# A diffusion layer on one core: the last bank in two halves, its second half squared on VectorE, epsilon as a column of the sums, and the mean's factor moved into the final norm's weights

## The chip, the core and the metric

The kernel runs on one core of one Trainium2 chip. The metric is the time of one execution in device microseconds, from the launch on the device to its end; lower is better. The profile's span runs from the first to the last instruction of the program and is a little shorter than that time.

## The reference, cut to what matters

One layer of a hybrid diffusion backbone on 256 latent tokens and 256 context tokens of width 2048 in float32: a SwiGLU feed-forward half step, a mixer (attention and mLSTM heads), a second feed-forward half step for the latent tokens, and a final RMS norm. The change touches the end of the second half step and the final norm alone:

```
D_MODEL = 2048; SEQ = 256; D_FF = 5632; RMS_EPS = 1e-6

def rms_norm(x, g):
    xf = x.astype(jnp.float32)
    y = xf * lax.rsqrt(jnp.mean(xf * xf, axis=-1, keepdims=True) + RMS_EPS)
    return (y * g.astype(jnp.float32)).astype(x.dtype)

def half_step_ffn(x, mod, i, g, w_up, w_down):
    h = adaln(x, g, mod, i)
    a, b = jnp.split(h @ w_up, 2, axis=-1)
    return x + 0.5 * mod[:, i + 2, None, :] * ((jax.nn.silu(a) * b) @ w_down)

    ...
    xl = half_step_ffn(xl, mod_l, 6, g_norm[l, 2], w_ffn2_up[l], w_ffn2_down[l])
    return rms_norm(xl, g_final)
```

## The kernel before

Every float32 matrix product is made of three products of rounded parts (`mm3`, L148 to L152). Each operand is split into a part `hi`, rounded by a ScalarE copy, and a rest `lo`, which VectorE gets by subtracting. TensorE then adds hi times hi, lo times hi and hi times lo in one PSUM bank. Weights arrive in tiles of 128 partitions by 2048 columns (1 MB, 8 KB per partition) and are split in two halves of 1024 columns (`split`, L120): L128 is the ScalarE copy, L129 the VectorE subtraction. There are three buffers for raw weights and four for each of hi and lo, so a split runs up to four halves ahead of TensorE. A buffer that TensorE has not yet read holds the split up, and a raw buffer that VectorE has not yet read holds up the next load on the DMA queue of SP.

The second feed-forward step works on 11 blocks of 512 hidden columns. The up projection of eight of them is done in the fast form `quad` (L2076 to L2175, banks X and Y) with chains of accumulating DMAs, issued by GpSimd, into the tiles `chain2` and `ra`. The down projection `down` adds pairs of blocks to `acc2`, a tile of 128 partitions, two token tiles and 2048 columns. Up and down are interleaved by hand (`sequence`, L2241). The order within an engine is otherwise made by a scheduler, which may move an instruction ahead of others unless it is pinned (`pin`, L337). An engine works through its instructions strictly in the order that is built.

When the last quad has used its chains, `before_final` (L2251) reuses their two buffers: `g8`, the gate row, and `gf`, the final norm's weights, each broadcast from one row to all 128 partitions by a DMA on SP (L2254, L2255). `gf` waits until the last split of the chain that lay in its buffer is done.

The end is `last2` (L2277). It loads the last block's down weights, four tiles of 2048 columns, and splits them (L2284 to L2290). Then for each of two token tiles `t` and each of four column blocks `cb` of 512:

- TensorE fills one bank with 12 products (`block`, L2200: four groups of 128 hidden columns, three products each), 512 columns wide.
- VectorE multiplies the bank by the gate (`half_gated`, L1030) and adds it to `acc2` (L2325).
- ScalarE squares the sum with an accumulator (`sumsq`, L163), which gives one column of the tile's four sums.
- VectorE multiplies the column block before it by `gf` (`gain`, L2293).

`ended` (L2295) closes a token tile: VectorE adds the four sums (L2298), multiplies by 1/2048 and adds epsilon (L2300), GpSimd raises to the power -1/2 (L2301), and ScalarE and VectorE scale the four column blocks (L2310, L2308; the very last one on VectorE with its gain, L2306). SP writes each block out (L2311). The first token tile's ending is laid between the banks of the second.

Of the kernel before, what the change touches and what calls it, by code (L numbers as in the profile page):

```python
# [9 lines left out]
F32 = mybir.dt.float32  # L10
# [3 lines left out]
AF = mybir.ActivationFunctionType  # L14
ALU = mybir.AluOpType
# [4 lines left out]
P = 128  # L20
D = 2048
# [25 lines left out]
CB = 512  # L47
NCB = D // CB
EPS = 1e-6
# [9 lines left out]
def tile_layer(ctx: ExitStack, tc: tile.TileContext, I: dict, out: bass.AP):  # L59
    nc = tc.nc  # L60
# [4 lines left out]
    sm = ctx.enter_context(pool(name="sm", bufs=2))  # L65
# [7 lines left out]
    def bank():  # L73
        return ps["mm"].tile([P, 512], F32, tag="mm", name="mm")

    def tbank():
        return ps["tr"].tile([P, 512], F32, tag="tr", name="tr")
# [20 lines left out]
    mhalf = cst.tile([P, 16], F32, name="mhalf")  # L98
# [17 lines left out]
    def raw_tile(n=2048):  # L116
        t = wp.tile([P, 2048], F32, tag="raw", name="raw", bufs=3)
        return t if n == 2048 else t[:, :n]
# [22 lines left out]
    def load_split(src, n=2048):  # L141
        raw = raw_tile(n)
        nc.sync.dma_start(raw, src)
        wt = split(raw, n)
        next(beside["load"], None)
        return wt
# [14 lines left out]
    def sumsq(dst, x, n=512):  # L161
        junk = sm.tile([P, 512], BF16, tag="junk", name="junk", bufs=1)
        scalar[0].activation(junk[:, :n], x, AF.Square, accum_out=dst)  # L163
# [173 lines left out]
    def pin(ins):  # L337
        tc.keep_in_program_order(ins)
# [58 lines left out]
    def drain(it):  # L397
        for _ in it:
            pass
# [62 lines left out]
    with pool(name="st", bufs=1) as st:  # L462
# [42 lines left out]
        def squares(s, t):  # L505

            ss4 = sm.tile([P, 4], F32, tag="ss4", name="ss4", bufs=4)
            for cb in range(NCB):
                xc = xs0[s, t][:, cb * CB : (cb + 1) * CB]
                if cb >= 2:  # L510
                    vector[0].scalar_tensor_tensor(junk[:, :CB], xc, 1.0, xc, op0=ALU.mult, op1=ALU.mult, accum_out=ss4[:, cb : cb + 1])
                else:
                    sumsq(ss4[:, cb : cb + 1], xc)
            return ss4

        def factor(ss4):
            s1 = sm.tile([P, 1], F32, tag="s1", name="s1")
            vector[0].tensor_reduce(s1, ss4, axis=AX.X, op=ALU.add)
            r = sm.tile([P, 16], F32, tag="rstd", name="rstd", bufs=4)[:, :1]
            vector[0].tensor_scalar(r, s1, 1.0 / D, EPS, op0=ALU.mult, op1=ALU.add)  # L520
            nc.gpsimd.tensor_tensor(r, r, mhalf[:, :1], op=ALU.pow)
            return r
# [91 lines left out]
        ss = squares(CTX, 0)  # L614
# [11 lines left out]
        r = factor(ss)  # L626
        for n, (s, t) in enumerate(((CTX, 1), (LAT, 0), (LAT, 1))):
            ss = squares(s, t)
# [4 lines left out]
            last, r = r, factor(ss)  # L633
# [98 lines left out]
    with pool(name="f1u", bufs=1) as f1u:  # L732
# [26 lines left out]
        for f in range(NPRE, FB):  # L759
            pab = []  # L760
            for ab in range(2):
                wt = load_split(I["w_up1"][f - NPRE, ab])
                b = bank()
# [168 lines left out]
        halves = [cBh[:, q, :] for q in range(2)]  # L932
# [95 lines left out]
    def half_gated(a, y, g, sign=1.0):  # L1028

        nc.vector.scalar_tensor_tensor(a, y, 0.5 * sign, g, op0=ALU.mult, op1=ALU.mult)  # L1030
# [8 lines left out]
    LAST = [(CTX, cb) for cb in (1, 3, 0, 2)] + [(LAT, cb) for cb in (2, 0, 3, 1)]  # L1039
# [207 lines left out]
    parts = [load_split(I["w_c"][g]) for g in range(2)]  # L1247
# [7 lines left out]
    with ExitStack() as mx:  # L1255
# [146 lines left out]
        def conv(b, ch, ns):  # L1402

            y = m1.tile([P, 512], F32, tag="cy", name="cy", bufs=3)[:, : ns * T]
            nc.scalar.activation(y, b, AF.Identity, scale=cwT[:, ch, 2:3], bias=cbT[:, ch : ch + 1])
            b3 = b.rearrange("p (s t) -> p s t", s=ns)
            y3 = y.rearrange("p (s t) -> p s t", s=ns)
            for j in (0, 1, 3, 4):
                o = j - 2
                src = slice(max(o, 0), T + min(o, 0))  # L1410
                dst = slice(max(-o, 0), T + min(-o, 0))
                nc.vector.scalar_tensor_tensor(y3[:, :, dst], b3[:, :, src], cwT[:, ch, j : j + 1], y3[:, :, dst], op0=ALU.mult, op1=ALU.add)  # L1412
            return y
# [39 lines left out]
        for h in range(NH):  # L1453
            b = bank()
# [4 lines left out]
            y = conv(b, 8 + h, 2)  # L1459
# [77 lines left out]
        for h in range(NH):  # L1537
            b = bank()[:, :T]
# [6 lines left out]
            y = conv(b, h, 1)  # L1545
# [11 lines left out]
        for w in range(2):  # L1557
            gs = gains[:, w, :].rearrange("p (a b d) -> p a b d", a=2, b=2)
            for t in range(2):
                nc.vector.tensor_tensor(rt[:, w, t, 0, :], rope[:, t, 0, :], gains[:, w, :], op=ALU.mult)  # L1560
                for b in range(2):
# [4 lines left out]
                        op=ALU.mult,  # L1566
# [315 lines left out]
        for cb in range(NCB):  # L1882
# [8 lines left out]
            c = slice(cb * CB, (cb + 1) * CB)  # L1891
# [36 lines left out]
    with f2x:  # L1928
# [4 lines left out]
        def sab_tile():  # L1933
            return f2.tile([P, CB], F32, tag="sab", name="sab")
# [22 lines left out]
        for f in range(NPRE, FB):  # L1957
            pab = []
            for ab in range(2):
                wt = load_split(I["w_up2"][f - NPRE, ab])  # L1960
                b = (tbank() if f == FB - 1 else bank())[:, :T]
# [17 lines left out]
        acc2 = f2b.tile([P, 2, D], F32, name="acc2", bufs=1)  # L1979
# [4 lines left out]
        LAST = NF // FB - 1  # L1984
# [212 lines left out]
                                nc.scalar.activation(sab[t], bs[t], AF.Silu)  # L2197
                    yield

        def block(b, n, wt, t, first=True, last=True):  # L2200

            tt = slice(t * P, (t + 1) * P)
            for j in range(FB):
                w = slice(j * CB, (j + 1) * CB)
                mm3(b, hids[n][0][:, j, tt], hids[n][1][:, j, tt], *wt(w), first and j == 0, last and j == FB - 1)
            return b

        late = {}
# [42 lines left out]
        def before_final():  # L2251
            late["g8"] = f3.tile([P, D], F32, tag="c0", name="g8")
            late["gf"] = f3.tile([P, D], F32, tag="c1", name="gf")
            nc.sync.dma_start(late["g8"], mod_rows[8][LAT, :].partition_broadcast(P))  # L2254
            nc.sync.dma_start(late["gf"], I["g_final"].partition_broadcast(P))  # L2255

        def quads():
            for n in QUADS:
                yield from quad(n)
# [17 lines left out]
        def last2():  # L2277

            parts = []
            for cb in range(NCB):  # L2280
                if cb >= 2:
                    parts.append(load_split(I["w_dn2"][LAST, cb]))
                    continue
                raw = raw_tile()  # L2284
                nc.sync.dma_start(raw, I["w_dn2"][LAST, cb])
                hi = f3.tile([P, 2048], F32R, tag=f"f{2 * cb}", name=f"hi{cb}")
                lo = f3.tile([P, 2048], F32R, tag=f"f{2 * cb + 1}", name=f"lo{cb}")
                nc.scalar.activation(hi, raw, AF.Copy)
                nc.vector.tensor_tensor(lo, raw, hi.bitcast(F32), op=ALU.subtract)
                parts.append(lambda w, hi=hi, lo=lo: (hi[:, w], lo[:, w]))  # L2290
            def gain(t, cb):
                a = acc2[:, t, cb * CB : (cb + 1) * CB]
                pin(nc.vector.tensor_tensor(a, a, late["gf"][:, cb * CB : (cb + 1) * CB], op=ALU.mult))  # L2293

            def ended(t, ss):  # L2295

                s1 = sm.tile([P, 1], F32, tag="s1", name="s1")
                pin(nc.vector.tensor_reduce(s1, ss, axis=AX.X, op=ALU.add))  # L2298
                r = sm.tile([P, 16], F32, tag="rstd", name="rstd", bufs=4)[:, :1]
                pin(nc.vector.tensor_scalar(r, s1, 1.0 / D, EPS, op0=ALU.mult, op1=ALU.add))  # L2300
                nc.gpsimd.tensor_tensor(r, r, mhalf[:, :1], op=ALU.pow)  # L2301
                for cb in (0, 2, 1, 3):
                    c = slice(cb * CB, (cb + 1) * CB)
                    a = acc2[:, t, c]
                    if t and cb == 3:
                        pin(nc.vector.scalar_tensor_tensor(a, a, r, late["gf"][:, c], op0=ALU.mult, op1=ALU.mult))  # L2306
                    elif cb >= 2:
                        pin(nc.vector.tensor_scalar(a, a, r, None, op0=ALU.mult))  # L2308
                    else:
                        nc.scalar.activation(a, a, AF.Copy, scale=r)  # L2310
                    nc.sync.dma_start(out[t * P : (t + 1) * P, c], a)  # L2311
                    if not t and not cb:
                        yield


            sss = [sm.tile([P, 4], F32, tag="ss4", name="ss4", bufs=4) for _ in range(2)]
            first = ended(0, sss[0])
            for t in range(2):
                for cb in range(NCB):
                    c = slice(cb * CB, (cb + 1) * CB)  # L2320
                    b = block(bank(), LAST, parts[cb], t)
                    a = acc2[:, t, c]
                    y = sab_tile()
                    half_gated(y, b, late["g8"][:, c])
                    nc.vector.tensor_tensor(a, a, y, op=ALU.add)  # L2325
                    sumsq(sss[t][:, cb : cb + 1], a)
                    if cb or t:
                        gain(*divmod(4 * t + cb - 1, 4))
                    if t:
                        steps(first)  # L2330
            drain(ended(1, sss[1]))

        last2()


# [93 lines left out]
```

## Time and profile before

| what | us |
| --- | --- |
| median of three runs | 2601.55 (2598.96 to 2601.9) |
| the profiled execution, its own time | 2600.28 |
| its span, first to last instruction | 2598.0 |
| mean granted TensorE clock | 0.996 |
| last product of TensorE starts | 2588.19 |
| scaling of the last token tile starts | 2591.89 |
| first and last write of the output issued | 2584.45 and 2593.80 |

Times in the views are microseconds from the start of the span. In a line of the timeline stand the start, the duration, the engine, the source line, the operation, the tiles (written from read), the shape and the count; in square brackets how long the engine was idle before and what ended that. A line of the grouped view ends with the total busy time, the mean nanoseconds of one, and the idle time before them. A line of the stage view gives the stretch, its length, then for TensorE, its weight loads (PEld), VectorE (DVE), ScalarE (ACT) and GpSimd (POOL) the busy time and count, then the granted clock, the share of the DMA engines and their GB/s.

### The profile page before, as it was taken

The numbers are of one execution on the slowest core, as the hardware profiler recorded it, in microseconds if no ns is written. First come the engines' busy times: TensorE is split into PE (matmuls) and PEld (weight loads), VectorE is DVE, ScalarE is ACT, GpSimd is POOL, SyncE is SP. The second block draws the span as 40 slices with busy tenths as digits, with TensorE's granted clock in tenths as the row PEclk, the third lists the DMA queues.
The fourth block names the chain that finished last, engine by engine and source line by source line (L and its number), as shares of the span: only waits on it lengthen the run. The fifth ranks groups of instructions, "written<-read, shape, count | busy, mean of one in ns | idle before, by whom it ended". The sixth has DMA issues, their size and how long they took to land. (4 is left out here: it accounts for less than half of the span.)

```text
span 2598.0 us, 34128 instructions
## 1 busy us (share of the span) xinstructions
PE 2574.4 (99%) x12670; PEld 2145.3 (83%) x12670; DVE 2172.5 (84%) x2864; ACT 1419.1 (55%) x1822; POOL 216.1 (8%) x265
## 2 busy tenths in 40 slices
PE   8999999999999999999999999999999999999998
PEld 5788888888888888888889989888898888888887
DVE  7788888878888788888887888798889888887887
ACT  4454444544445565444454448456486676666664
POOL 0000000100000100000110000120000000000001
PEclk8999999999999999999999999999999999999999
DMA  9889999999999989989987897676768988989976
GB/s 391 346 220 265 269 286 268 263 276 285 262 287 262 281 246 242 218 216 224 229 254 261 296 321 242 235 279 215 267 239 244 276 267 259 271 275 275 260 230 174
DMA packets 127078, 680.51 MB, mean 262 GB/s; under 512 B 14136, under 2 KB 16696, under 8 KB 64832
## 3 DMA queue, kind: packets, MB, share of 16 engines
q1 hardware_dynamic: 98400, 492.73, 50.8%
q0 software_dynamic: 28512, 185.61, 36.5%
q8 instruction: 99, 1.62, 0.2%
q14 instruction: 67, 0.55, 0.1%
HBM read 660.39 MB, written 17.89 MB: 261 GB/s over the span
## 5 line engine op out<-in xcount | busy, mean ns | idle before, releaser
L128 ACT ACTIVATE hi<-raw 128x1024 fp32r<-128x1024 f32 (+2 forms) x500 | 519.0, 1042 | 424.2 <-PE mm L152 308.3
L129 DVE TENSOR_TENSOR lo<-raw,hi 128x1024 fp32r<-128x1024 f32 (+2 forms) x488 | 584.9, 1206 | 144.4 <-ACT hi L128 119.3
L128 ACT ACTIVATE hi<-chain 128x1024 fp32r<-128x1024 f32 x336 | 355.6, 1060 | 303.5 <-PE mm L152 191.4
L129 DVE TENSOR_TENSOR lo<-chain,hi 128x1024 fp32r<-128x1024 f32 x336 | 407.8, 1222 | 115.1 <-ACT hi L128 108.8
L152 PE MATMUL mm<-hi,hhi 128*128 128x512 f32 (+3 forms) x1024 | 394.0, 385 | 0.0
L152 PE MATMUL mm<-lo,hhi 128*128 128x512 f32 (+3 forms) x1024 | 387.0, 378 | 0.2 <-DVE lo L129 0.2
L152 PE MATMUL mm<-hi,hlo 128*128 128x512 f32 (+3 forms) x1024 | 386.4, 377 | 0.0
L208 DVE SCALAR_TENSOR_TENSOR junk<-sraw,cBh 128x1024 fp8e5<-128x1024 f32 x192 | 234.4, 1221 | 16.5 <-DMA sraw<-in_w_mt 14.3
L152 PEld LDWEIGHTS mm<-lo,hhi 128*128 128x128 f32 x1024 | 192.5, 188 | 34.5 <-DVE lo L129 0.6
L152 PEld LDWEIGHTS mm<-hi,hhi 128*128 128x128 f32 x1024 | 192.6, 188 | 31.0
L152 PEld LDWEIGHTS mm<-hi,hlo 128*128 128x128 f32 x1024 | 192.8, 188 | 30.7
L129 DVE TENSOR_TENSOR lo<-ra,hi 128x1024 fp32r<-128x1024 f32 x96 | 117.1, 1223 | 36.8 <-ACT hi L128 32.2
L128 ACT ACTIVATE hi<-ra 128x1024 fp32r<-128x1024 f32 x96 | 101.9, 1062 | 65.5 <-PE mm L152 49.0
L152 PE MATMUL mm<-lo,hid2h 128*128 128x512 f32 x352 | 137.1, 389 | 0.0
L152 PE MATMUL mm<-hi,hid2h 128*128 128x512 f32 x352 | 137.0, 389 | 0.0
L152 PE MATMUL mm<-hi,hid2l 128*128 128x512 f32 x352 | 136.9, 389 | 0.0
L152 PE MATMUL mm<-hi,sumshl 128*128 128x512 f32 x400 | 123.2, 389 | 0.0
L208 DVE SCALAR_TENSOR_TENSOR sr<-sr,cBl 128x1024 f32<-128x1024 f32 x84 | 102.2, 1224 | 15.1 <-DMA sr<-in_w_mt 13.6
L731 POOL DMA_DIRECT2D chain<-in_w_up1b x60 | 53.0, 884 | 729.4 <-DVE lo L129 729.4
L152 PE MATMUL mm<-hi,sumshh 128*128 128x512 f32 x352 | 108.4, 389 | 0.0
L152 PE MATMUL mm<-hhi,hi 128*128 128x512 f32 (+1 forms) x288 | 101.4, 352 | 0.0
L152 PE MATMUL mm<-hhi,lo 128*128 128x512 f32 (+1 forms) x288 | 99.0, 344 | 0.0
(490 smaller groups left out, 5457.0 us busy)
## 6 DMA issues: line engine op xcount, KB each, us to landing
raw<-in_w_dn SPq DMA_DIRECT2D x70, 1024.0 KB, 7.1
chain<-in_w_up1b POOLq DMA_DIRECT2D x60, 1024.0 KB, 10.2
sraw<-in_w_mt SPq DMA_DIRECT2D x96, 512.0 KB, 8.1
sr<-in_w_mt SPq DMA_DIRECT2D x81, 512.0 KB, 5.5
raw<-in_w_up1b SPq DMA_DIRECT2D x40, 1024.0 KB, 8.1
mraw<-in_w_m SPq DMA_DIRECT2D x32, 1024.0 KB, 8.1
raw<-in_w_up2b SPq DMA_DIRECT2D x32, 1024.0 KB, 8.1
chain<-in_w_dn POOLq DMA_DIRECT2D x30, 1024.0 KB, 8.5
```

Source lines behind the costliest of these rows:

```text
L128: scalar[0].activation(hi, src, AF.Copy)
L129: vector[0].tensor_tensor(lo, src, hi.bitcast(F32), op=ALU.subtract)
L152: tensor[0].matmul(out_ap, s, m, start=first and not n, stop=last and n == 2, skip_group_check=skip)
L208: ins = nc.vector.scalar_tensor_tensor(junk() if junk else raw, raw, 1.0, cB[s], op0=ALU.mult, op1=ALU.mult, accum_out=mT[:, i, s, kt, h : ...
L731: accum = lambda dst, src: nc.gpsimd.dma_start(dst, src, accum_op=ALU.add)
```

## The change

Four edits, all at the end.

- The last bank (second token tile, last column block) is filled as two banks of 256 columns, first columns 0 to 255, then 256 to 511, each with its own 12 products, gate and addition. The first half is squared by ScalarE as before. The second half is squared by VectorE, in one operation with an accumulator.
- The sums of a token tile have six columns instead of four. The fifth is the second half's sum (zero for the first token tile), the sixth holds 2048 times epsilon. GpSimd fills both by memsets, which the built program places at the start of GpSimd's instructions, between the two selects that make the identity.
- The step that multiplied by 1/2048 and added epsilon (L2300 before) is gone: the six columns are added and go straight to the power -1/2.
- The missing factor, the square root of 2048, is multiplied into `gf` by a ScalarE copy right behind its load in the code.

The additions to `acc2` are now pinned; on VectorE their order is the old one. The line numbers behind the edits move: L2325 becomes L2328, L2293 becomes L2294, L2298 becomes L2299, L2288 becomes L2289; L2301 to L2311 stay. The new lines are L2256 (the factor), L2318 and L2319 (the memsets), L2341 (VectorE's square).

```diff
-        def block(b, n, wt, t, first=True, last=True):
+        def block(b, n, wt, t, first=True, last=True, c0=0):
 
             tt = slice(t * P, (t + 1) * P)
             for j in range(FB):
-                w = slice(j * CB, (j + 1) * CB)
+                w = slice(j * CB + c0, j * CB + c0 + b.shape[1])
...
             nc.sync.dma_start(late["gf"], I["g_final"].partition_broadcast(P))
+            nc.scalar.activation(late["gf"], late["gf"], AF.Copy, scale=D ** 0.5)
...
                 r = sm.tile([P, 16], F32, tag="rstd", name="rstd", bufs=4)[:, :1]
-                pin(nc.vector.tensor_scalar(r, s1, 1.0 / D, EPS, op0=ALU.mult, op1=ALU.add))
-                nc.gpsimd.tensor_tensor(r, r, mhalf[:, :1], op=ALU.pow)
+                nc.gpsimd.tensor_tensor(r, s1, mhalf[:, :1], op=ALU.pow)
...
-            sss = [sm.tile([P, 4], F32, tag="ss4", name="ss4", bufs=4) for _ in range(2)]
+            sss = [sm.tile([P, 6], F32, tag="ss6", name="ss6", bufs=2) for _ in range(2)]
+            for ss in sss:
+                nc.gpsimd.memset(ss[:, 4:5], 0.0)
+                nc.gpsimd.memset(ss[:, 5:6], D * EPS)
             first = ended(0, sss[0])
+
+            def finished(t, cb, c0, n):
+                c = slice(cb * CB + c0, cb * CB + c0 + n)
+                b = block(bank()[:, :n], LAST, parts[cb], t, c0=c0)
+                a = acc2[:, t, c]
+                y = sab_tile()[:, :n]
+                half_gated(y, b, late["g8"][:, c])
+                pin(nc.vector.tensor_tensor(a, a, y, op=ALU.add))
+                return a
+
             for t in range(2):
                 for cb in range(NCB):
-                    c = slice(cb * CB, (cb + 1) * CB)
-                    b = block(bank(), LAST, parts[cb], t)
-                    a = acc2[:, t, c]
-                    y = sab_tile()
-                    half_gated(y, b, late["g8"][:, c])
-                    nc.vector.tensor_tensor(a, a, y, op=ALU.add)
-                    sumsq(sss[t][:, cb : cb + 1], a)
+                    halves = t == 1 and cb == NCB - 1
+                    a = finished(t, cb, 0, CB // 2 if halves else CB)
+                    sumsq(sss[t][:, cb : cb + 1], a, a.shape[-1])
                     if cb or t:
                         gain(*divmod(4 * t + cb - 1, 4))
+                    if halves:
+                        a = finished(t, cb, CB // 2, CB // 2)
+                        y = sab_tile()[:, : CB // 2]
+                        pin(nc.vector.scalar_tensor_tensor(y, a, 1.0, a, op0=ALU.mult, op1=ALU.mult, accum_out=sss[t][:, 4:5]))
                     if t:
                         steps(first)
```

## The prediction

> **What bounds the kernel now.** First the page, then the stage view (busy time by stretch), then the timelines of the end.
>
> ```profile
> PE 2574.4 (99%) x12670; PEld 2145.3 (83%) x12670; DVE 2172.5 (84%) x2864; ACT 1419.1 (55%) x1822; POOL 216.1 (8%) x265
> ```
> ```profile
> 2515.70:2588.60 72.90, 72.87 (x329) 59.93 (x327) 56.96 (x70) 32.63 (x42) 7.52 (x9) 1.00 0.63 188
> ```
>
> TensorE is busy for 99% of the span, and in the last 73 us before its end it is busy for 72.87 of 72.90 us. That stretch has no hole that could swallow a delay: what makes TensorE late before 2515 makes the end late by as much. After TensorE there is only a chain of small steps. Here it is on VectorE, then on ScalarE and GpSimd:
>
> ```profile
> 2586.62 0.69 DVE L2325 TENSOR_TENSOR acc<-acc,sab 128x512 f32<-128x512 f32 x1
> 2587.23 0.69 DVE L2293 TENSOR_TENSOR acc<-acc,gf 128x512 f32<-128x512 f32 x1
> 2588.61 0.69 DVE L1030 SCALAR_TENSOR_TENSOR sab<-mm,g 128x512 f32<-128x512 f32 x1 [0.70 <-PE mm L152]
> 2589.34 0.69 DVE L2325 TENSOR_TENSOR acc<-acc,sab 128x512 f32<-128x512 f32 x1
> ...
> 2590.88 0.16 DVE L2298 TENSOR_REDUCE s<-ss 128x1 f32<-128x4 f32 x1 [0.25 <-ACT junk L163]
> 2591.07 0.15 DVE L2300 TENSOR_SCALAR rstd<-s 128x1 f32<-128x1 f32 x1
> 2591.89 0.49 DVE L2308 TENSOR_SCALAR acc<-acc,rstd 128x512 f32<-128x512 f32 x1 [0.67 <-POOL rstd L2301]
> ```
> ```profile
> 2590.12 0.63 ACT L163 ACTIVATE junk<-acc 128x512 bf16<-128x512 f32 x1 [1.99 <-DVE acc L2325]
> 2590.66 0.19 ACT L163 ACTIVATION_READ_ACCUMULATOR junk<-acc 128x1 f32 x1
> ```
> ```profile
> 2591.30 0.55 POOL L2301 TENSOR_TENSOR rstd<-rstd,mhalf 128x1 f32<-128x1 f32 x1 [7.63 <-DVE rstd L2300]
> ```
>
> Read: the last bank is gated at 2588.61, added at 2589.34, squared by ScalarE at 2590.12, summed at 2590.88, given its mean and epsilon at 2591.07, raised to -1/2 at 2591.30. Only at 2591.89 can the last row be scaled and written out. A dependent VectorE step of 512 columns follows after 0.73 us (2588.61 to 2589.34), an independent one after 0.61 (2586.62 to 2587.23).
>
> **The end, part by part.** Can TensorE do the last bank as two halves at no cost?
>
> ```profile
> 2585.69 0.39 PE L152 MATMUL mm<-hi,hid2h 128*128 128x512 f32 x1
> ...
> 2588.19 0.39 PE L152 MATMUL mm<-lo,hid2h 128*128 128x512 f32 x1
> ```
> ```profile
> 1392.72 0.28 PE L152 MATMUL mm<-hi,hlo 128*128 128x256 f32 x1
> ...
> 1394.28 0.28 PE L152 MATMUL mm<-lo,hhi 128*128 128x256 f32 x1
> ```
>
> The bank's 12 products of 512 columns start 0.227 us apart (2.50 over 11). Elsewhere 14 products of 256 columns with the same weight loads start 0.120 apart (1.56 over 13). So 24 of them end at 2585.69 + 23 x 0.120 + 0.28 = 2588.73, 0.15 later than now (2588.58), and the first half at 2587.29. VectorE then works, in the order of the built program, through gate A, add A, gain of column block 2 (512 wide), gate B, add B, square B, sum.
>
> ```profile
> L1510 DVE SCALAR_TENSOR_TENSOR E<-mm,E 128x256 f32<-128x256 f32 x16 | 6.6, 415 | 0.7 <-POOL E L1495 0.6
> ```
> ```profile
> L129 DVE TENSOR_TENSOR lo<-raw,hi 128x1024 fp32r<-128x1024 f32 x464 | 563.9, 1222 | 137.3 <-ACT hi L128 112.3 <-PE mm L1429 9.9 <-PE mm L1705 1.7
> ...
> L208 DVE SCALAR_TENSOR_TENSOR junk<-sraw,cBh 128x1024 fp8e5<-128x1024 f32 x192 | 234.4, 1221 | 16.5 <-DMA sraw<-in_w_mt 14.3
> ...
> L208 DVE DVE_READ_ACCUMULATOR junk<-sraw,cBh 128x1 f32 x192 | 15.9, 83 | 0.0
> ```
>
> 256 columns take 0.415 us where 512 take 0.69, so each step shrinks by 0.27: 0.46 dependent, 0.34 independent. Gate A starts when the gain at 2587.23 lets go, 2587.84; add A 2588.30; gain 2588.64; gate B 2589.25 (its bank ended at 2588.73); add B 2589.71; square 2590.17; its accumulator is read 0.34 later and takes 0.08, so the sum starts at 2590.62 and ends at 2590.78. ScalarE's square of half A begins near 2588.7 and is long done. The step at L2300 is gone: POOL follows the sum 0.08 us later (now 2591.22 to 2591.30), takes 0.55, and scaling starts at 2591.45 instead of 2591.89. The end gains **0.44 us**. No row shows a 256-wide square with accumulator. If the halves saved nothing, the sum would come 0.27 x 5 later and the end lose 0.9; if the accumulator read were free, it would gain 0.5. I stay at the L1510 row, with 0.2 to 0.55 as its range.
>
> The Trainium skill, page "Vector Engine (DVE) Microarchitecture Reference", section "Points that are easy to get wrong", says that such an operation with two non-bf16 SBUF sources runs at half rate, no port being left for the accumulator. By it the square would take an estimated 0.27 us more and the gain be 0.17. The trace disagrees: with accumulator 1.221 us, L129 without one 1.222.
>
> **Epsilon.** Four one-column memsets appear on POOL, between the two selects that make the identity.
>
> ```profile
> 0.94 0.11 POOL L100 MEMSET mhalf<- 128x16 f32 x1
> ...
> 1.91 0.29 POOL L104 TENSOR_SCALAR_AFFINE_SELECT ident<-ident 128x128 f32<-128x128 f32 x1
> ```
> ```profile
> 2.98 0.28 PE L467 MATMUL tr<-ident,cc 32*128 32x32 f32 x1 [2.98 <-ACT cc L191]
> ```
>
> At 0.11 each they delay the identity from 2.20 to 2.64 at most. Its first user starts at 2.98 and waits for ScalarE. Cost nothing; without that cover, 0.44.
>
> **The factor in gf.** This is the term that decides. The new ScalarE instruction at L2256 stands, in the built program, behind the last copy of L2105 and ahead of six splits of L128, two of ra and four of raw. It waits for gf's load, which before nobody needed until 2576.
>
> ```profile
> L2255 SPq DMA_DIRECT2D gf<-in_g_final x1: 327/327/327, 2502.1 to 2502.1; - x1
> ...
> DMA to landing us min/median/max: 10.6/10.6/10.6
> ```
> ```profile
> 2506.39 0.60 ACT L2105 ACTIVATE ca<-X 128x512 f32<-128x512 f32 x1 [0.54 <-DVE cy L2077]
> 2508.93 1.06 ACT L128 ACTIVATE hi<-ra 128x1024 fp32r<-128x1024 f32 x1 [1.93 <-PE mm L152]
> ...
> 2553.40 1.92 ACT L2288 ACTIVATE hi<-raw 128x2048 fp32r<-128x2048 f32 x1 [2.03 <-DMA raw<-in_w_dn]
> 2555.22 1.99 ACT L128 ACTIVATE hi<-raw 128x1024 fp32r<-128x1024 f32 x2
> ```
> ```profile
> 2510.02 2.60 DVE L129 TENSOR_TENSOR lo<-ra,hi 128x1024 fp32r<-128x1024 f32 x2 [2.53 <-ACT hi L128]
> ```
> ```profile
> 2512.76 0.39 PE L152 MATMUL Y<-lo,h2hi 128*128 128x512 f32 x1
> 2512.99 0.39 PE L152 MATMUL Y<-hi,h2hi 128*128 128x512 f32 x1
> ...
> 2513.44 0.39 PE L152 MATMUL Y<-lo,h2hi 128*128 128x512 f32 x1
> ```
>
> ScalarE would reach L2256 at 2507.0; gf lands at 2502.1 + 10.6 = 2512.7. Nothing ahead of that load changes, so I keep the landing. A pass over 2048 columns lets the next one start 1.82 later (2553.40 to 2555.22): the split of ra starts at 2514.5 instead of 2508.93. VectorE's lo follows 1.09 behind (2508.93 to 2510.02) at 2515.6 and ends 1.22 later, 2516.8. TensorE wants this lo at 2513.44, the third product of the second tile. **It stands still for 3.4 us**: drained at 2513.15, two products at 2515.6, the rest from 2516.8. The lo's behind come at most 1.22 apart and are wanted 6 products, 1.36, apart, so they add nothing. The later loads of raw move back with their buffers, but so does TensorE. The delay is the landing time less 2509.3, for any landing after that.
>
> A hole of that size has a second price: the clock.
>
> ```profile
> 2507.00:2512.70 5.70, 5.70 (x27) 4.72 (x26) 2.94 (x3) 3.17 (x3) 0.00 (x0) 1.00 1.01 423
> ...
> 36.65:40.07 3.42, 1.39 (x18) 0.77 (x19) 2.09 (x3) 0.19 (x1) 0.00 (x0) 1.00 1.02 424
> 40.07:43.48 3.41, 3.41 (x13) 2.71 (x12) 2.05 (x8) 1.66 (x3) 0.00 (x0) 0.50 1.01 428
> ...
> 2586.40:2589.80 3.40, 2.17 (x10) 1.48 (x8) 2.63 (x5) 0.72 (x2) 0.00 (x0) 1.00 0.54 183
> ```
>
> A stretch of 3.41 us with 1.39 us of TensorE work was followed by one of 3.41 us at clock 0.50; one with 2.17 was not followed by any, until the end. Laid over the hole (idle from 2513.15 to 2515.6 and from 2516.05 to 2516.8), a 3.41 us stretch holds under 1.39 us of work if it starts between 2511.8 and 2514.3: 2.5 of 3.41, some 70% of its positions, and more if the bound lies between 1.39 and 2.17. Half clock for 3.41 us loses 1.7, less what of the hole is still in it: I take **1.5** (0 to 1.7).
>
> The Trainium skill, "TensorE: Matmul & The Clock Gate", section "What's actually happening", halves the clock after at least one idle window of about 3.4 us. Read strictly, no window here is wholly idle, and the time would be the second rival's. The 1.39 row speaks against that reading.
>
> **Sum** against the profiled execution (2600.28 us, span 2598.0): 3.4 + 1.5 - 0.44 = +4.5, **2604.7 us**. The median of the three runs lies 1.3 above that execution. Differences under 0.2%, 5.2 us, are about what a measurement of this kernel cannot tell from none; +4.5 is 0.17%, so the forecast is no measurable change, on the slow side.
>
> **Rivals.**
> 1. *No stall.* gf lands by 2509.3, 7.2 us after its issue. The end's 0.44 alone remains: 2599.8. For it: loads of mraw, as large, land in 8.1 (row below), which would leave 0.9. Against: the measured 10.6, with the DMA engines at share 1.01 around it. Chance 0.12.
> 2. *Stall, no slow clock*, the windows lying luckily: 3.4 - 0.44, 2603.2. Chance 0.17.
> 3. *Slower than can be missed*: gf lands later. The DMA engines are full there, and every us of landing is a us of TensorE. From 2513.4 on, 11.3 us after the issue, the sum passes 5.2; with 1.5 us more it is 2606.2. Against: same queue, same neighbours. Chance 0.11.
> 4. *Addresses.* The new tag makes pool sm 64 bytes longer, and in the built program most later pools (chain, mraw, acc2) start 64 bytes further on, off multiples of 256.
>
> ```profile
> sraw<-in_w_mt SPq DMA_DIRECT2D x96, 512.0 KB, 8.1
> sr<-in_w_mt SPq DMA_DIRECT2D x81, 512.0 KB, 5.5
> ...
> mraw<-in_w_m SPq DMA_DIRECT2D x32, 1024.0 KB, 8.1
> ```
>
> If a row of 8 KB then touched one more block of 256, the 32 loads of mraw (33.6 MB at 424 GB/s, 79 us, with TensorE waiting) would take 2.5 us more: 2607.2. Against: sr already lies 192 bytes off in the kernel before, and lands no later than sraw, which lies on a multiple. Chance 0.07.
>
> **How the numbers follow.** The forecast has 0.53. Rivals 3 and 4 (0.18) are slower by over 0.2%, and with the scatter of runs a fifth of the forecast's cases too: 0.29. Faster by over 0.2%: 0.02, scatter on rival 1. Within: 0.69. The range goes from rival 2 less 1.3 us of scatter, 2601.9, to rival 3 plus 1.7, 2607.9; it leaves out rivals 1 and 4.
>
> **What would show it.** In the changed profile: L2256 idle some 5.7 us until DMA gf; a hole of 3 us on TensorE near 2513, lo as its releaser; one stretch of about 3.4 us at clock 0.50 behind it; TensorE's end to the scaling shortened from 3.3 to about 2.7 us; 256-wide products 0.12 apart. I am wrong if L2256 starts before 2510, if TensorE closes the hole later, or if the first 120 us grow.

## The result, and the profile after

The changed kernel takes **2616.47 us** (median of six runs, 2613.34 to 2617.4). The kernel before, run beside it, takes 2600.26 us (2597.96 to 2603.78). The ratio is 1.0061 with a 95% interval of 1.0051 to 1.0071: slower by about 16 us. The forecast was 2604.7 us, and its range ended at 2607.9.

The page of the changed kernel shows TensorE's total:

```profile
span 2614.9 us, 34160 instructions
...
PE 2589.3 (99%) x12682; PEld 2145.6 (82%) x12682; DVE 2174.5 (83%) x2866; ACT 1420.7 (54%) x1823; POOL 215.4 (8%) x269
```

The span grew by 16.9 us, and TensorE's busy time alone by 14.9. A stall is idle time and could not do that. Most of the loss is therefore in products that take longer, and idle time is the small part of it. Where the loss grows is read off two ScalarE copies that both kernels have. Here are the last copy of L2095 near 1992 us and the one of L2105 ahead of the new instruction, from the timeline of the kernel before and then of the kernel after:

```profile
1992.36 0.58 ACT L2095 ACTIVATE ca<-Y 128x512 f32<-128x512 f32 x1
```
```profile
1991.63 0.58 ACT L2095 ACTIVATE ca<-Y 128x512 f32<-128x512 f32 x1
...
2515.39 0.60 ACT L2105 ACTIVATE ca<-X 128x512 f32<-128x512 f32 x1 [0.53 <-DVE cy L2077]
2521.76 1.91 ACT L2256 ACTIVATE gf<-gf 128x2048 f32<-128x2048 f32 x1 [5.77 <-DMA gf<-in_g_final]
```

At L2095 the changed kernel is 0.73 us ahead. At L2105, which stood at 2506.39 before, it is 9.00 behind. So **9.73 us are lost before the new ScalarE instruction has even begun**, in a stretch in which no instruction was changed. In between the loss grows evenly. It comes from the products themselves. These are TensorE's timelines of the same stretch of work, two products apart, before and after:

```profile
2299.71 0.39 PE L152 MATMUL mm<-hi,hid2h 128*128 128x512 f32 x1
...
2302.43 0.39 PE L152 MATMUL Y<-hi,h2hi 128*128 128x512 f32 x1
```
```profile
2304.13 0.40 PE L152 MATMUL mm<-hi,hid2l 128*128 128x512 f32 x1
...
2306.93 0.40 PE L152 MATMUL Y<-hi,h2lo 128*128 128x512 f32 x1
```

Each fence spans 12 steps from one product to the next: 2.72 us before, 2.80 after, so 226.7 ns against 233.3. In a row such as mm<-hi,hid2h the first name read (hi) is the moving operand, a half of a weight tile, and the second (hid2h) is the stationary one, which TensorE loads ahead of the product. The tiles h2hi, h2lo, hid2h and hid2l are the only stationary ones in pool f2, apart from 16 transposes; here they are called f2's tiles. With them in the stationary place stand 2004 products of 512 columns in the changed kernel; 1513 of these start between the two ScalarE copies, and 1513 times 6.5 ns is 9.8 us. Products of 512 columns whose stationary tile lies in another pool kept their 227 ns. In the built program f2's tiles begin at byte 67136 of each partition instead of 67072. That is 64 bytes further, because the new column tile lengthened pool sm; the pool of the weight halves hi and lo stayed where it was, at byte 6656.

Behind L2256 stand the stall and the slow clock. VectorE's row, TensorE's rows and the stage view of the changed kernel:

```profile
2524.64 2.36 DVE L129 TENSOR_TENSOR lo<-ra,hi 128x1024 fp32r<-128x1024 f32 x2 [8.16 <-ACT hi L128]
```
```profile
2521.99 0.39 PE L152 MATMUL Y<-lo,h2hi 128*128 128x512 f32 x1
2524.67 0.50 PE L152 MATMUL Y<-hi,h2hi 128*128 128x512 f32 x1 [2.29 <-ACT hi L128]
...
2525.93 0.80 PE L152 MATMUL Y<-lo,h2hi 128*128 128x512 f32 x1 [0.52 <-DVE lo L129]
2526.52 0.63 PE L152 MATMUL Y<-hi,h2hi 128*128 128x512 f32 x1
2526.95 0.63 PE L152 MATMUL Y<-hi,h2lo 128*128 128x512 f32 x1
```
```profile
2521.84:2525.25 3.41, 1.12 (x5) 0.40 (x3) 0.60 (x1) 3.41 (x3) 0.00 (x0) 1.00 0.20 82
2525.25:2528.66 3.41, 2.89 (x8) 2.16 (x8) 3.41 (x4) 3.25 (x4) 0.00 (x0) 0.50 0.00 0
2528.66:2532.08 3.42, 3.42 (x10) 2.65 (x9) 3.23 (x4) 1.70 (x3) 0.00 (x0) 0.50 0.54 146
2532.08:2605.00 72.92, 72.92 (x331) 59.29 (x330) 54.56 (x67) 30.70 (x39) 7.51 (x9) 1.00 0.60 179
```

The two holes are about those forecast, 2.29 us until hi and 0.52 until lo (2.45 and 0.75 in the prediction). The granted clock falls to 0.50 behind them, products are 0.43 apart, and this lasts for two stretches of 3.41 us, not one. What stall and clock cost together is read off an addition L2226 behind them, before and after, and the first product of the last bank shows how the lag goes on (2585.69 before):

```profile
2531.49 0.69 DVE L2226 TENSOR_TENSOR acc<-acc,mm 128x512 f32<-128x512 f32 x1 [0.62 <-PE mm L152]
```
```profile
2547.19 0.69 DVE L2226 TENSOR_TENSOR acc<-acc,mm 128x512 f32<-128x512 f32 x1 [0.71 <-PE mm L152]
```
```profile
2602.99 0.28 PE L152 MATMUL mm<-hi,hid2h 128*128 128x256 f32 x1
```

The addition comes 15.70 us later than before. From L2105 on, stall and clock together with about 100 products by f2's tiles thus cost 15.70 - 9.00 = 6.70 us; without these products, at 6.5 ns each, it is some 6.0. TensorE then never waits again, as the last row of the stage view shows. At the last bank it is 17.30 us late: another 1.60 over some 240 products by f2's tiles, 6.7 ns each.

The end, in VectorE's and TensorE's timelines of the changed kernel:

```profile
2605.92 0.68 DVE L2294 TENSOR_TENSOR acc<-acc,gf 128x512 f32<-128x512 f32 x1
2606.52 0.42 DVE L1030 SCALAR_TENSOR_TENSOR sab<-mm,g 128x256 f32<-128x256 f32 x1
2606.97 0.42 DVE L2328 TENSOR_TENSOR acc<-acc,sab 128x256 f32<-128x256 f32 x1
2607.43 0.43 DVE L2341 SCALAR_TENSOR_TENSOR sab<-acc 128x256 f32<-128x256 f32 x1
2607.78 0.08 DVE L2341 DVE_READ_ACCUMULATOR sab<-acc 128x1 f32 x1
2607.97 0.16 DVE L2299 TENSOR_REDUCE s<-ss 128x1 f32<-128x6 f32 x1
2608.80 0.49 DVE L2308 TENSOR_SCALAR acc<-acc,rstd 128x512 f32<-128x512 f32 x1 [0.67 <-POOL rstd L2301]
```
```profile
2605.70 0.28 PE L152 MATMUL mm<-lo,hid2h 128*128 128x256 f32 x1
```

TensorE ends at 2605.98, and the scaling starts 2.82 us later. Before it was 3.31. The changed tail does what it was expected to do, and the steps are those of the prediction in their order.

### The profile page after: what moved, and what is told of

The parts are those of the page before. It is cut to its first block, busy times and chain, and to the rows that moved or that the text cites. A ratio compares the mean times of both kernels' runs of the same rounds, so it can differ in the third digit from the quotient of the medians.

```text
span 2614.9 us, 34160 instructions
## 1 busy us (share of the span) xinstructions
PE 2589.3 (99%) x12682; PEld 2145.6 (82%) x12682; DVE 2174.5 (83%) x2866; ACT 1420.7 (54%) x1823; POOL 215.4 (8%) x269
## 5 line engine op out<-in xcount | busy, mean ns | idle before, releaser
L208 DVE SCALAR_TENSOR_TENSOR junk<-sraw,cBh 128x1024 fp8e5<-128x1024 f32 x192 | 234.4, 1221 | 16.9 <-DMA sraw<-in_w_mt 14.5
L152 PE MATMUL mm<-hi,hid2h 128*128 128x512 f32 (+1 forms) x356 | 140.3, 394 | 0.0
L152 PE MATMUL mm<-lo,hid2h 128*128 128x512 f32 (+1 forms) x356 | 140.2, 394 | 0.0
L152 PE MATMUL mm<-hi,hid2l 128*128 128x512 f32 (+1 forms) x356 | 140.1, 393 | 0.0
```

What stands on the lines that cost most here:

```text
L152: tensor[0].matmul(out_ap, s, m, start=first and not n, stop=last and n == 2, skip_group_check=skip)
L208: ins = nc.vector.scalar_tensor_tensor(junk() if junk else raw, raw, 1.0, cB[s], op0=ALU.mult, op1=ALU.mult, accum_out=mT[:, i, s, kt, h : ...
```

## The experiments

Three things had to be told apart: the loss in f2's products, the stall with its slow clock, and the tail. The theory is that the 64 bytes cause the first and the copy of gf the second, and that nothing else is lost. The rival is that the steady loss comes from something else in the change. A second question is what about the 64 bytes matters: the stationary tile's own start, or its distance from the moving tile. The medians of the first four experiments stand against 2603.44 us, the kernel before run beside them (23 runs).

**The changed kernel with its pools where they were.** Line 188 is a pad of 64 bytes at the head of pool sm; without it the wider column tile moves nothing behind it.

```diff
-    sm.tile([P, 16], F32, name="smpad", bufs=1)
```

> The changed kernel without the 64-byte pad at the head of pool sm, so that with the wider column tile every later pool stands where it stood before; nothing else differs from the changed kernel. Theory A (the products whose stationary tile lies in pool f2 start 6.7 ns later each once these tiles begin 64 bytes further): the steady growth between 2000 and 2510 us is gone, the products by h2hi, h2lo, hid2h and hid2l are back at about 226.8 ns apart, and the time is before + 3.2 (stall) + 1.5 to 3.4 (one or two slow windows) - 0.4 (end), so 2604 to 2607 us. Theory B (the growth comes from something else that the change does, such as the new copy or the order of the instructions): 2615 to 2617 us, with those products still 233 ns apart.

Measured: 2606.32 us, ratio 1.0016 (1.0007 to 1.0026), so 1.8 to 6.8 us above before, where the changed kernel was 13 to 18 above. From the timelines of this kernel:

```profile
1993.55 0.58 ACT L2095 ACTIVATE ca<-Y 128x512 f32<-128x512 f32 x1
```
```profile
2507.58 0.60 ACT L2105 ACTIVATE ca<-X 128x512 f32<-128x512 f32 x1 [0.53 <-DVE cy L2077]
2514.09 1.91 ACT L2256 ACTIVATE gf<-gf 128x2048 f32<-128x2048 f32 x1 [5.92 <-DMA gf<-in_g_final]
```
```profile
2537.93 0.69 DVE L2226 TENSOR_TENSOR acc<-acc,mm 128x512 f32<-128x512 f32 x1 [0.63 <-PE mm L152]
```
```profile
2514.57:2517.98 3.41, 0.73 (x2) 0.30 (x2) 1.00 (x1) 3.41 (x4) 0.00 (x0) 1.00 0.13 53
2517.98:2521.39 3.41, 3.13 (x7) 2.51 (x8) 3.41 (x4) 2.87 (x3) 0.00 (x0) 0.50 0.00 0
2521.39:2524.80 3.41, 3.41 (x16) 2.82 (x15) 3.41 (x5) 1.69 (x2) 0.00 (x0) 1.00 0.63 209
```

The two ScalarE copies are 1.19 us later than before, both of them: between them nothing is lost any more. The stall is there, with one slow stretch, and the addition L2226 comes 6.44 us later than before. The steady loss is the addresses and nothing else in the change.

**The kernel before with f2 moved.** No instruction changes; an unused tile of 16 numbers stands ahead of f2's tiles. The two pools behind them, hs and f2b, move along; neither holds a tile of these 512-column products.

```diff
-        f2 = f2x.enter_context(pool(name="f2", bufs=2))
+        f2 = f2x.enter_context(pool(name="f2", bufs=2)); f2.tile([P, 16], F32, name="f2pad", bufs=1)
```

> The kernel before with one unused tile of 64 bytes per partition ahead of the tiles of pool f2: no instruction changes, only the tiles of f2 and of the few pools behind it on the same side begin 64 bytes further. Theory A (start address of the stationary tile): about 2000 products by 6.7 ns, +13.4 us, so 2613 to 2615 us, with no stall and no slow window at the end. Theory B (not the addresses of f2): within 1 us of before.

Measured: 2615.04 us, ratio 1.0051 (1.0036 to 1.0067). The same two copies in its timeline:

```profile
1992.89 0.58 ACT L2095 ACTIVATE ca<-Y 128x512 f32<-128x512 f32 x1
...
2516.62 0.60 ACT L2105 ACTIVATE ca<-X 128x512 f32<-128x512 f32 x1 [0.54 <-DVE cy L2077]
```

They are 0.53 and 10.23 us later than before. The loss between them is 9.70, where the changed kernel has 9.73. An unused tile of 64 bytes costs this kernel half a per cent.

**The copy of gf alone**, in the kernel before, with a factor of 1.

```diff
+            nc.scalar.activation(late["gf"], late["gf"], AF.Copy, scale=1.0)
```

> The kernel before with the one ScalarE copy of gf at the place where the change puts it, with a factor of 1, so that the norm stays as it was; no address changes. Theory A (the copy costs its stall and its slow clock and nothing else): +3.2 and +1.5 to +3.4, so 2604.5 to 2607 us, all of it after 2510 us. Theory B (the copy is behind the whole loss): 2613 us or more. If the stall were covered: 2600 us.

Measured: 2610.39 us, ratio 1.0029 (1.0018 to 1.0041), more than expected. From the timelines of its profiled execution:

```profile
2512.80 0.60 ACT L2105 ACTIVATE ca<-X 128x512 f32<-128x512 f32 x1 [0.53 <-DVE cy L2077]
```
```profile
2542.96 0.69 DVE L2226 TENSOR_TENSOR acc<-acc,mm 128x512 f32<-128x512 f32 x1 [0.63 <-PE mm L152]
```

This execution, at 2611.53 us, is already 6.41 us behind at L2105, ahead of the copy. Two single slow stretches of clock lie there (957 and 1838 us), with 4.2 and 3.3 us lost around them; no run here shows what caused them, nor whether the other five runs had them. From L2105 to the addition L2226 the lag grows from 6.41 to 11.47 us. So stall and clock cost **5.06 us** here, and by the same two rows of the kernel without the pad, 5.25. Both have one slow stretch. The time of the whole run told this apart badly; the trace's two rows did it.

**The copy of gf late.** The changed kernel without the pad, the copy moved behind the last split of hid3's weights.

```diff
-            nc.scalar.activation(late["gf"], late["gf"], AF.Copy, scale=D ** 0.5)
...
             first = ended(0, sss[0])
+            pin(nc.scalar.activation(late["gf"], late["gf"], AF.Copy, scale=D ** 0.5))
```

> The changed kernel without the 64-byte pad, and with the copy of gf moved from behind its transfer's issue to the tail, where ScalarE reaches it behind the last split of hid3 and ahead of the first square of the final norm. Theory A (addresses, stall and clock are the whole loss): none of the three is left, and the shortened end stands alone, -0.3 to -0.6 us, 2599.6 to 2600.0 us beside 2600.2 for before on the same chip. Rival: the copy in its new place delays a square or an eviction of the tail by its 1.9 us, and the time is 2601 to 2602 us.

Measured: 2602.73 us, ratio 1.0001 (0.9992 to 1.0010). In ScalarE's timeline the copy lies in a hole:

```profile
2573.99 1.90 ACT L2321 ACTIVATE gf<-gf 128x2048 f32<-128x2048 f32 x1
2578.09 0.63 ACT L163 ACTIVATE junk<-acc 128x512 bf16<-128x512 f32 x1 [2.20 <-DVE acc L2328]
```

The first square still waits 2.20 us for VectorE, so the copy delays nothing. The clock stays full until TensorE's end. This is the change without both of its faults, and it can't be told from the kernel before: the tail's half microsecond is 0.02%. Its scaling starts 2.77 us behind TensorE's end.

**How far f2 may lie.** The same unused tile with 32, 128, 256 and 192 bytes (8, 32, 64 and 48 numbers), one run each, beside the kernel with 64 above.

```diff
-        f2 = f2x.enter_context(pool(name="f2", bufs=2))
+        f2 = f2x.enter_context(pool(name="f2", bufs=2)); f2.tile([P, 8], F32, name="f2pad", bufs=1)
```

> The kernel before with an unused tile of 32 bytes per partition ahead of pool f2's tiles. Theory A with a boundary of 64 bytes or more: the products by h2hi, h2lo, hid2h and hid2l are about 233 ns apart (perhaps more, if the loss grows as the start lies further off), 2613 to 2615 us. Theory A with a boundary of 32 bytes: 226.8 ns and 2600 us; but 64 bytes would then be harmless too, so this is ruled out already if the 64-byte kernel is slow.

> The kernel before with an unused tile of 128 bytes per partition ahead of pool f2's tiles. If the boundary that counts is 128 bytes: the products by f2's tiles are at 226.8 ns and the time is 2600 us. If it is 256 or 512 bytes: 233 ns and 2613 to 2615 us.

> The kernel before with an unused tile of 256 bytes per partition ahead of pool f2's tiles. If the boundary that counts is 128 or 256 bytes: 226.8 ns and 2600 us. If it is 512 bytes (the size of one 128-column stationary slice in four-byte numbers): 233 ns and 2613 to 2615 us.

> The kernel before with an unused tile of 192 bytes per partition ahead of pool f2's tiles. The stationary tiles lie 192 bytes behind the moving ones, modulo 256, which is the same as the 64 bytes the other way round that the kernel with the wider constants' pad had. Theory A2 (the distance modulo 256 counts): the same pattern as there, three products of a group at about 231, 226 and 229.5 ns, mean 229, so +4 us for some 1960 products, about 2604. Theory A1 (any start off 256 costs the same): 233 ns and +13 us, about 2614.

| f2 moved by (bytes) | start to start, ns (mean of 1963 products by f2's tiles, neighbours alike) | time, us | before beside it |
| --- | --- | --- | --- |
| 0 | 227 | 2600.28 (profiled) | |
| 32 | 233.2 | 2614.12 | 2602.86 |
| 64 | 233.4 | 2615.04 | 2603.44 |
| 128 | 232.5 | 2615.81 | 2602.86 |
| 192 | 229.0 | 2606.11 | 2600.76 |
| 256 | 227 | 2599.56 | 2602.86 |

The period is 256 bytes: 128 is as bad as 64, and 256 is free. The kernel before bears it out: the distances from moving to stationary tile in its 512-column products take every multiple of 256 up to 2048, and each of the eight groups is 226.7 to 227.7 ns apart. Within it the loss isn't one step: at 192 it is a third of that at 64. TensorE's timeline of the kernel with 192 bytes shows 11 steps in 2.52 us, 229 ns each:

```profile
2299.87 0.39 PE L152 MATMUL mm<-hi,hid2h 128*128 128x512 f32 x1
...
2302.39 0.39 PE L152 MATMUL mm<-lo,hid2h 128*128 128x512 f32 x1
```

**Own start or distance?** The constants' pad 64 bytes wider moves all pools of the left side.

```diff
-    cst.tile([P, 40], F32, name="cstpad")
+    cst.tile([P, 56], F32, name="cstpad")
```

> The kernel before with the constants' pad 64 bytes wider, so that the pools on the left side, the one with the moving weight halves hi and lo among them, begin 64 bytes further, while pool f2 and the other pools on the right stay where they are. Theory A1 (only the start of the stationary tile counts): the products by f2's tiles stay at 226.8 ns, and only those whose stationary tile itself moved change. Theory A2 (the distance between stationary and moving tile counts): the products by f2's tiles and by all other right-hand tiles go to about 233 ns, and the time grows by far more than 13 us. Theory A3 (the start of the moving tile counts too): every product by hi and lo is slower.

The expectation has a slip: f2 lies on the left side too, and moved along with the weight halves. Measured: 2614.42 us in one run, beside 2602.86. Products by form in the kernel before, then in this one (the last figures are the total busy time, the mean ns of one, and the idle time):

```profile
L152 PE MATMUL mm<-hi,n1h 128*128 128x512 f32 x160 | 62.2, 389 | 0.0
L152 PE MATMUL mm<-hi,n1l 128*128 128x512 f32 x160 | 62.2, 389 | 0.0
L152 PE MATMUL mm<-lo,n1h 128*128 128x512 f32 x160 | 62.2, 389 | 0.0
```
```profile
L152 PE MATMUL mm<-hi,hid2h 128*128 128x512 f32 x352 | 137.2, 390 | 0.0
...
L152 PE MATMUL mm<-hi,n1h 128*128 128x512 f32 x160 | 63.0, 394 | 0.0
L152 PE MATMUL mm<-lo,n1h 128*128 128x512 f32 x160 | 62.8, 392 | 0.0
...
L152 PE MATMUL mm<-hi,n1l 128*128 128x512 f32 x160 | 62.2, 389 | 0.0
```

The products by hid2h, whose two operands both start 64 bytes off, lose nothing (227 ns apart). Those by n1h and n1l lose, though their stationary tiles still start on a multiple of 256: only the moving side moved. They are about 231, 226 and 229.5 ns apart, 229.1 over all 6709 products of this kind. Counted from the moving tile, the stationary one lies 192 bytes further on, modulo 256. That is why the kernel with 192 bytes was expected at 229, and it came there. The time grew by less than theory A2 had expected of so many products, since at this distance one loses 2 ns and not 6.5.

The same trace, joined with the addresses of the built program, holds two more groups. The 768 products of 512 columns that have a weight half as the stationary tile (mm<-hhi,hi and its like) came to distance 64, and they are 233.2 ns apart. The 384 products of the same kind with 256 columns, also at 64, went the other way: 114.2 ns apart (1587.05 to 1588.31 is 11 steps), where the kernel before has 119.6 (1576.23 to 1577.55). So the loss isn't one of every width: at 256 columns the same shift gains 5 ns.

The last step moves both sides.

```diff
-    edge.tile([P, 56], F32, name="edge")
+    edge.tile([P, 40], F32, name="edge")
...
-    cst.tile([P, 40], F32, name="cstpad")
+    cst.tile([P, 56], F32, name="cstpad")
```

> The kernel before with all of its pools, left and right, 64 bytes further (the constants' pad 64 bytes wider, the pad at the right-hand edge 64 bytes narrower). Every tile lies off a multiple of 256 bytes now, but the distance from the moving to the stationary tile of each 512-column product is a multiple of 256 bytes again. Theory A2 (the distance counts): all products at 227 ns, the time that of before within 0.2%. Theory A1 (the stationary tile's own start counts): every one of some 9800 products 6.5 ns slower, +60 us. If the loads of the weights cared about 64 bytes: the first 120 us grow by 2.5 us.

Measured: 2601.59 us beside 2600.76, ratio 1.0004 (0.9994 to 1.0013). The operands of these products all start off a multiple of 256 bytes, the products are 227.2 ns apart, and nothing is lost; 32 loads of mraw land in 7.5 us beside 8.1. **In the 512-column products the distance between the two operands counts, modulo 256, not where either lies.**

**One slow stretch or two?** The changed kernel once more.

> The changed kernel once more, to see whether the slow clock behind the stall lasts one stretch of 3.41 us or two. In the profile of it that is there, the stretch that began 0.6 us before the stall's last wait was followed by a second slow one; in the two kernels with the same copy there was one. If the position of the stretches decides: one or two, as they fall. If the changed kernel always has two: two again. The rest as before: 2614 to 2618 us, products by f2's tiles at 233 ns.

Measured: 2618.23 us, with one slow stretch. The stage view, with the stretch ahead of it:

```profile
2525.55:2528.96 3.41, 1.01 (x4) 0.49 (x4) 1.47 (x2) 3.41 (x4) 0.00 (x0) 1.00 0.04 14
2528.96:2532.37 3.41, 3.41 (x9) 2.64 (x9) 3.41 (x4) 2.40 (x3) 0.00 (x0) 0.50 0.00 0
2532.37:2535.78 3.41, 3.41 (x16) 2.74 (x15) 3.30 (x5) 1.69 (x2) 0.00 (x0) 1.00 0.75 250
```

So the second stretch doesn't come every time. By the same two rows (2518.65 and 2548.79) stall, clock and the 100 products of f2 cost 5.04 us here, where the profiled execution has 6.70. That the way the stretches lie over the hole decides it is argued and not shown. Behind the stall a slow stretch in which TensorE worked 3.13 or 3.41 of 3.41 us was followed by the full clock, and the one with 2.89 (the short wait for lo fell into it) by another slow one. This is no general rule: in the kernel before, a slow stretch with 3.41 us of work (19.59 to 23.00) was followed by a slow one too.

**The tail without the halves**, on top of the kernel with the late copy.

```diff
-                    halves = t == 1 and cb == NCB - 1
+                    halves = False
```

> The kernel with the late copy of gf and no pad, but with the last bank again as one of 512 columns, squared by ScalarE; epsilon stays a column of the sums and the factor stays in gf. By the step-by-step sum, what remains is the step at L2300 that is gone, worth 0.2 us: from TensorE's end to the scaling 3.1 us, beside 3.31 in the kernel before and 2.77 with the halves. If instead most of the gain came from epsilon and the factor: 2.8 us.

Measured: TensorE's end at 2587.77, scaling at 2590.89, **3.12 us**; the whole run took 2598.7, which says nothing at this size. VectorE's timeline:

```profile
2588.53 0.69 DVE L2328 TENSOR_TENSOR acc<-acc,sab 128x512 f32<-128x512 f32 x1
...
2590.07 0.16 DVE L2299 TENSOR_REDUCE s<-ss 128x1 f32<-128x6 f32 x1 [0.25 <-ACT junk L163]
2590.89 0.49 DVE L2308 TENSOR_SCALAR acc<-acc,rstd 128x512 f32<-128x512 f32 x1 [0.67 <-POOL rstd L2301]
```

The step that is gone is worth 0.19, the halves with VectorE's square 0.35, less the 0.15 by which TensorE ends later.

## Why the prediction was wrong

**The step that failed** is the rival of addresses, and with it the sentence "Nothing ahead of that load changes". The prediction saw that most pools move by 64 bytes, and asked only what that costs a DMA. It gave 2.5 us and a chance of 0.07. The runs show nothing of it in the loads (the first 120 us didn't grow, and mraw lands in 7.7 us, 8.1 before). They show 6.5 ns on each 512-column product whose moving and stationary tiles no longer lie a multiple of 256 bytes apart: 9.73 us before the new instruction, some 12 in all (the kernel with f2 alone moved is 11.6 above the one before). No row of the kernel before could have priced it: its 512-column products with weights all have distance zero modulo 256, and the nearest others, 95 of 416 columns at 128, are 189.1 ns apart against 188.3 at zero. But the address list of the two builds showed which operand moved against which, and a bound for it belonged into the range: 1% on 2004 products is already 4.5 us. The two DMA sizes that were compared, sr and sraw, were evidence on DMAs only.

**The stall was right.** gf landed 10.7 us after its issue (10.6 assumed), L2256 waited 5.77 us (some 5.7), and with one slow stretch stall and clock cost 5.06 and 5.25 us in two kernels, and some 4.4 in the second execution of the changed one, whose L2256 waited 5.35; the sum was 3.4 + 1.5 = 4.9. In the two kernels, what remains beside the clock, at up to 1.7, is 3.4 or a little more.

**The clock's term was right in kind and too narrow in size.** One half-clock stretch was taken as the worst. In the profiled execution there were two, and stall and clock came to some 6.0. Nor do the traces bear out a bound between 1.39 and 2.17 us of work: the clock fell behind stretches with 0.73, 1.01 and 1.12 us here, but in the kernel before also behind one with 2.91 us (12.76 to 16.17), which the prediction overlooked. The Trainium skill, page "TensorE: Matmul & The Clock Gate", section "What's actually happening", halves the clock after at least one idle window. In its strict reading this rule fails, since none of these stretches was idle. The same section calls the window free-running. The two executions of the changed kernel, with one and two stretches, agree with that.

**The tail was right.** 2.82 us from TensorE's end to the scaling was forecast as about 2.7, against 3.31, so 0.49 gained there. The last bank takes TensorE 2.99 us from first start to end, where it took 2.88, so its end comes 0.11 later by the narrower products (0.15 in the kernel with the late copy), and 0.38 of the forecast 0.44 is left. VectorE's square took 0.43 us for 256 columns, as the L1510 row had it (0.415), not at half rate. The one slip is 0.1 between the accumulator's read and the sum.

**The memsets were right.** They start at 1.80 to 1.90 us and the first product at 2.90, no later than before.

Without the addresses the changed kernel is at 1.0007 to 1.0026 of the kernel before, and the forecast 2604.7 of 2600.28 is 1.0017. What the prediction worked out came out close to it, up to the number of slow stretches; what it didn't price was larger than all of it.

## What to carry to other kernels

When a change adds or widens a tile, list which tiles move by how much, and look at each kind of matrix product: in the 512-column products of this kernel the moving and the stationary tile should keep a distance that is a multiple of 256 bytes. Taking 64 bytes of padding out repaired it here. When a kernel gets slower, compare the start-to-start times of its products by stationary tile: the few that changed their pace point to the tile that moved. An instruction placed next to a load in the code is on its engine's queue there: put it where that engine has a hole, as the late copy was, or it holds up everything behind it until the load lands.

## What the runs showed of the hardware

The pace of a 512-column fp32r product depends on where its two operands lie to each other: at distance 0 modulo 256 bytes a product follows the last one after 227 ns, at 32, 64 or 128 after 232.5 to 233.4, at 192 after 229. At 256 columns the sign is another: 119.6 to 120.0 ns at distance 0, 117.8 at 192, and 113.4 to 117.8 at 64, the 117.8 in the last bank of the changed kernel.

The Trainium skill, page "TensorE: Matmul & The Clock Gate", section "Step-by-step: what each phase is for", gives TensorE two independent read ports, and has the next weights' load take no read bandwidth from the running product. By that alone the distance should not matter, and these runs measure a cost of up to 6.5 ns, 3%, which depends on the addresses alone.

It is no collision with another engine. In the kernel with f2 moved by 64 bytes, 89 products by f2's tiles ran while ScalarE and VectorE did nothing, and 82 while no DMA packet was under way and GpSimd did nothing. Both groups are 233.7 ns apart; the same groups of the kernel before (80 and 82) are 226.7 and 226.6.

That TensorE's own two reads meet in the same blocks of the memory at some distances would explain the period, but no run here shows the blocks, nor which of the reads waits, and it stays open. Open too is why products of 256 columns gain where those of 512 lose.
